# A decoder layer on one core: more of the gated layer made ahead, prompt rows weighed in pairs, sums taken from PSUM product by product

## The chip, the cores and the metric

The kernel runs on one core of a Trainium2 chip. The metric is the time on the device in microseconds. Times are given as the median of several runs, and one further execution was recorded by the profiler.

## The reference

One inference step of a decoder layer of width 2048, for one prompt of 512 new tokens and eight sample requests of 8 tokens each, 576 tokens together. The layer's input is normed by rows, `u = rms_norm(x, g_mix) @ w_in`, and `u` is shared out to three mixers: a short gated convolution (512 columns), a Mamba-2 state-space mixer (512) and sparse attention (1024). The attention has 16 query heads on 4 key heads and three branches: over compressed blocks of keys, over selected blocks and over a window of 512. A sample request has 1024 past positions in paged caches, whose raw rows are compressed by a small network. Queries and keys are normed by heads. The three outputs are normed, merged and sent through the output projection, and a gated feed-forward layer ends the step:

```
merged = concat(rms_norm(y_a), rms_norm(y_b), rms_norm(y_c))
x = x + merged @ w_out
h = rms_norm(x, g_ffn)
x = x + (silu(h @ w_gate) * (h @ w_up)) @ w_down      # d_ff = 5632
```

New cache rows, convolution tails and states are outputs as well. All data is float32.

## The kernel before

The token axis (576 columns, 288 in each half) is the free axis of nearly every matmul. A float32 product is made of three matmuls of parts: `hi` times `hi`, `hi` times `lo` and `lo` times `hi`. ScalarE makes the rounded part of a weight chunk (`whi`, `fhi`), VectorE the remainder (`wlo`, `flo`). A projection job (`run_group`, L405) makes 128 output columns from 16 row blocks: 16 x 3 x 2 = 96 matmuls of 128 x 288. There are 21 jobs for keys, values, queries and gates (`jobs1`), 12 for the state-space mixer (`jobs2`), 12 for the short convolution (`jobs3`). The two of `jobs1` that make the raw keys run while x is turned and split; `begin` also makes the row scales `rstdB` there (L334, L637), through a power on GpSimd and transposes on TensorE. The helpers record every operation under one line: L93 is ScalarE's, L96 a two-input operation, L105 one with a scalar.

Everything else of the token mixers is side work in Python generators. `Pump` (L44) holds them; each reports by `tick(ns)` a planned cost and yields. After each row block, `run_group` calls `pump.run(369.0 * halves * ratio)`, which steps generators until that much cost is used up. So ratio says how densely side work is written between projection matmuls: 0.8 for `jobs1`, 0.95 for `jobs2`, 1.1 for `jobs3` (L1653). The generator `chain` goes through the compression of the caches (`compress`, with `k_cmp_norm`, L680), sample attention, prompt attention and the merge of the attention's output (`merge_c`, L1609); `pump.drain(main)` writes what is left of it behind the last projection job. The finishing steps of projections are generators as well: `norm_T` (L467) norms a query or key by squares (ScalarE), a matmul with a block of ones, Ln and Exp on ScalarE, and one multiplication; `kv_finish` (L485) turns and stores a key or value. The framework below the kernel then places each engine's instructions in an order of its own that follows the written one loosely, and sets the semaphores.

The prompt attention (L1559) goes through four query heads `r` of a group: `turn(r)` transposes four tiles of probabilities on TensorE and copies each out of PSUM, `apply` multiplies them with values into `o`.

The gated layer (L1893) multiplies with w_gate and w_up by seven products of half-size blocks in place of eight. For each of 44 blocks `g` (gate and up by turns) and both chunks `c` of rows, matmuls (L1915) make products 1, 2, 6, 4, 3, 7, 5 into PSUM pieces P["1"] to P["7"]: 24 matmuls a product, 12 in each chunk. 1 and 2 have tiles `pt` of their own, 5 has `po`; 6 and 4 are the halves of one `pg` tile, 3 and 7 of another; only in blocks 1 to NE - 1 do 6 and 4 have `pt` tiles of their own. After the second chunk VectorE adds the pieces to `u` and `w_`, which then go through Silu, or (odd g) are multiplied on GpSimd with the Silu of the block before and stored to `g_d`. `prep(i)` splits the weights one item ahead.

For the first NE = 8 blocks products 1 and 2 are made ahead by `jobsE` (two jobs a block, 24 matmuls each) and kept in DRAM as `U_d`. Ten of these jobs (2 x NA) run while the second half of the norm is made, `norm_b` with `pair` (L1790), at ratio 0.6; the other six run inside the first item at 0.8. `pair` makes the combinations of the normed inputs that the products need, most on VectorE, three of each on GpSimd (`G`). The down projection follows; its first inputs are four stored rows, split by `g_in` into `ghl`.

The stages lie at these times of the trace (us): start to 64; projections with side work to 1142; the output projection to 1401; norm and early products to 1477; gated layer to 2401; down projection to the end.

## Time and profile before

| | us |
|---|---|
| median of 3 runs (lowest, highest) | 2980.53 (2979.23, 2984.72) |
| profiled execution | 2985.47 |
| its span | 2983.7 |
| TensorE (PE) busy | 2860.0 (96%) |
| VectorE (DVE) busy | 1942.6 (65%) |
| ScalarE (ACT) busy | 1204.7 (40%) |
| GpSimd (POOL) busy | 579.2 (19%) |

The granted clock of TensorE has a mean of 0.981. PE is the matmuls, PEld the weight loads that overlap them. The idle time of an engine that is not the bottleneck costs nothing; TensorE's idle time, wherever it lies, is time that a better order could use.

### The profile page before, as it was taken

The page shows a single profiled execution, that of the slowest core. Times are in us where ns is not written, and L with a number is a line of the kernel's source. Part 1 is how long each engine was busy: PE and PEld are TensorE (multiplying, and loading weights), DVE is VectorE, ACT ScalarE, POOL GpSimd, SP SyncE. Part 2 cuts the span into 40 slices and gives each one's busy share as a digit, 9 for nine tenths or more (in the row PEclk, how much of TensorE's full clock was granted, in tenths as well). Part 3 has the DMA queues.
Part 4 walks back from the last instruction along what each step waited for, and adds up shares of the span by engine and source line. Part 5 has one row for each costly group of instructions (what it writes and reads, how often), then busy time and mean ns, then how long its engine had stood idle before and what let it go on. Part 6 is the DMA issues. An engine that isn't in the chain of part 4 may idle for free.

```text
span 2983.7 us, 57369 instructions
## 1 busy us (share of the span) xinstructions
PE 2860.0 (96%) x22294; PEld 2756.0 (92%) x22294; DVE 1942.6 (65%) x3982; ACT 1204.7 (40%) x2287; POOL 579.2 (19%) x632
## 2 busy tenths in 40 slices
PE   7999998777999999999899999999999999999999
PEld 6989997666888899999899999999999999999999
DVE  5674774334786776668998888888888863343332
ACT  4463662222455542245544444444444431222222
POOL 3342424444343321112211110110110100000000
PEclk9999998888999999999999999999999999999999
DMA  7444434554524117366553333333333272332333
GB/s 235 121 128 126 104 81 122 151 152 153 125 54 90 49 47 196 110 199 180 158 182 124 112 108 107 109 109 108 108 108 108 83 245 86 117 114 82 96 100 94
DMA packets 476056, 364.07 MB, mean 122 GB/s; under 512 B 69738, under 2 KB 436305, under 8 KB 475785
## 3 DMA queue, kind: packets, MB, share of 16 engines
q1 hardware_dynamic: 452056, 299.99, 34.5%
q0 software_dynamic: 20944, 55.13, 6.3%
q10 hardware_dynamic: 2784, 5.29, 0.5%
q8 instruction: 176, 2.88, 0.4%
q14 instruction: 96, 0.78, 0.1%
HBM read 307.61 MB, written 50.61 MB: 120 GB/s over the span
## 4 chain that ended last, share of the span: by engine, by line
PE 55%; DVE 2%; ACT 0%; issue 0%; DMA 0%; POOL 0%; DVEq 0%; ACTq 0%; POOLq 0%; SPq 0%
PE pg L431 23%; PE pg L1915 17%; PE pt L1915 9%; PE po L1915 5%; DVE wlo L96 1%; PE pt L128 0%; DVE x L105 0%; PE pt L120 0%; DVE X L96 0%; DVE raw L96 0%; DVE x L96 0%; PE pt L431 0%; DMA raw<-in_w_gate_dram 0%; PE po L120 0%; ACT X L93 0%
## 5 line engine op out<-in xcount | busy, mean ns | idle before, releaser
L93 ACT ACTIVATE whi<-raw 128x512 fp32r<-128x512 f32 x729 | 458.1, 629 | 938.7 <-PE pg L431 575.2
L96 DVE TENSOR_TENSOR wlo<-raw,whi 128x512 fp32r<-128x512 f32 x729 | 505.5, 695 | 351.2 <-ACT whi L93 334.1
L431 PE MATMUL pg<-ghl,whi 128*128 128x288 f32 x2816 | 495.2, 296 | 2.4 <-DVE ghl L96 2.1
L431 PEld LDWEIGHTS pg<-ghl,whi 128*128 128x128 f32 x2816 | 414.9, 189 | 3.2 <-DVE ghl L96 2.8
L431 PE MATMUL pg<-hhi,whi 128*128 128x288 f32 (+1 forms) x1440 | 343.9, 320 | 9.7 <-issue 4.3
L431 PE MATMUL pg<-hlo,whi 128*128 128x288 f32 (+1 forms) x1440 | 326.2, 306 | 6.4 <-issue 4.2
L431 PE MATMUL pg<-hhi,wlo 128*128 128x288 f32 (+1 forms) x1440 | 324.1, 304 | 2.7 <-issue 2.6
L431 PE MATMUL pg<-ghl,wlo 128*128 128x288 f32 x1408 | 302.5, 296 | 0.0
L431 PEld LDWEIGHTS pg<-hhi,whi 128*128 128x128 f32 (+1 forms) x1440 | 238.0, 197 | 26.4 <-issue 20.0
L1915 PE MATMUL pt<-X,fhi 128*128 128x288 f32 x1280 | 258.5, 296 | 0.0
L431 PEld LDWEIGHTS pg<-hlo,whi 128*128 128x128 f32 (+1 forms) x1440 | 241.8, 196 | 11.8 <-issue 8.0
L1915 PE MATMUL pg<-X,fhi 128*128 128x288 f32 x1232 | 246.9, 295 | 0.8 <-ACT fhi L93 0.8
L431 PEld LDWEIGHTS pg<-hhi,wlo 128*128 128x128 f32 (+1 forms) x1440 | 241.4, 195 | 4.4 <-issue 4.0
L96 POOL TENSOR_TENSOR u<-u 128x576 f32<-128x576 f32 x44 | 69.8, 1588 | 822.8 <-DVE u L96 702.8
L431 PEld LDWEIGHTS pg<-ghl,wlo 128*128 128x128 f32 x1408 | 226.1, 189 | 0.0
L93 ACT ACTIVATE fhi<-wr 128x512 fp32r<-128x512 f32 x225 | 142.2, 632 | 189.4 <-PE pt L1915 106.4
L96 DVE TENSOR_TENSOR flo<-wr,fhi 128x512 fp32r<-128x512 f32 x225 | 197.4, 877 | 13.5 <-ACT fhi L93 11.1
L1915 PEld LDWEIGHTS pt<-X,fhi 128*128 128x128 f32 x1280 | 205.8, 188 | 0.0
L1915 PEld LDWEIGHTS pg<-X,fhi 128*128 128x128 f32 x1232 | 197.8, 188 | 1.1 <-ACT fhi L93 1.1
L431 PE MATMUL pg<-S,whi 128*128 128x288 f32 x1024 | 194.8, 298 | 0.0
L96 DVE TENSOR_TENSOR x1T<-pg,x1T 128x576 f32<-128x576 f32 x96 | 72.6, 757 | 183.0 <-PE pg L431 183.0
L1915 PE MATMUL pt<-X,flo 128*128 128x288 f32 x640 | 189.2, 296 | 0.0
(1324 smaller groups left out, 5964.3 us busy)
## 6 DMA issues: line engine op xcount, KB each, us to landing
wr<-in_w_gate_dram SPq DMA_DIRECT2D x88, 512.0 KB
wr<-in_w_up_dram SPq DMA_DIRECT2D x88, 512.0 KB
raw<-in_w_down_dram SPq DMA_DIRECT2D x176, 256.0 KB
raw<-in_w_in_dram SPq DMA_DIRECT2D x144, 256.0 KB
raw<-in_w_out_dram SPq DMA_DIRECT2D x64, 256.0 KB
g_d<-u POOLq DMA_DIRECT2D x44, 288.0 KB
u<-g_d SPq DMA_DIRECT2D x40, 288.0 KB
raw<-in_w_in_dram SPq DMA_DIRECT2D x64, 128.0 KB
```

The source lines that it names most:

```text
L93: S.activation(out, in_, func, bias=bias, scale=scale, accum_out=accum)
L96: (eng or V).tensor_tensor(out, a, b, op=op)
L431: PE.matmul(ps[:m, s, :HALF], w[:, k, :m], x[:, s * HALF:(s + 1) * HALF], start=(k0 + k == 0 and n == 0), stop=(k0 + k == n_k - 1 and n == 2))
L1915: PE.matmul(P[n], w[:, k, :], xx, start=(j == 0 and q_ == 0), stop=(j == 7 and q_ == 2))
```

## The change

It does these things:

- NE goes from 8 to 12 and NA from 5 to 8; the early jobs beside `norm_b` run at ratio 0.45 in place of 0.6, and `pair`'s three GpSimd operations go to VectorE.
- `row_scales` becomes a generator with one pause. The two raw-key jobs leave PSUM by a plain copy, and `kv_finish` multiplies by the scales when they are there.
- `norm_T` pauses twice, for 900 each, in place of once for 700.
- `k_cmp_norm` takes the power by Ln and Exp on ScalarE in place of GpSimd.
- In prompt attention, where the row has up to 256 keys, two transposed tiles share a PSUM bank and one copy, the rows are applied in pairs with two more pauses, and `o` is taken later.
- `merge_c` has all multiplications on VectorE; the ratios of `jobs2` and `jobs3` go to 0.85 and 1.05.
- In the gated layer the sums are written between the products: those of P1 and P2 after product 2, P6's after 6, P7's, P4's and P3's after 7. The last block's P5 sums, its multiplications and stores come after the first four splits of the down projection.

```diff
@@ -141,8 +141,8 @@
     SQ = 3
     PF = 3
     XSB = 2
-    NE = 8
-    NA = 5
+    NE = 12
+    NA = 8
     QLB = 1
     EVB = 5
     CRB = 5
@@ -334,7 +334,10 @@
     def row_scales():
         tt(ssq, ssq2[:, 0], ssq2[:, 1], OP.add)
         rsqrt_small(ssq, 1.0 / D)
+        tick(2500)
+        yield
         spread(rstdB, ssq)
+        ready.add("scales")
 
 
     R_GF, R_GO, R_CA, R_CB, R_BB, R_QN, R_KN, NR1 = 0, 16, 32, 44, 76, 84, 85, 88
@@ -471,8 +474,9 @@
         sq, sh, sl_ = evt(T), evt(T, F32R), evt(T, F32R)
         act(sq, u, AF.Square)
         split(sh, sl_, sq)
-        tick(700)
-        yield
+        for _ in range(2):
+            tick(900)
+            yield
         for s in range(2):
             sl = slice(s * HALF, (s + 1) * HALF)
             ps = pt()
@@ -482,7 +486,12 @@
         act(sq, sq, AF.Exp, scale=-0.5)
         stt(out, u, gain, sq, OP.mult, OP.mult)
 
-    def kv_finish(br, kv, p, u):
+    def kv_finish(br, kv, p, u, raw=False):
+        if raw:
+            while "scales" not in ready:
+                yield
+            tt(u, u, rstdB, OP.mult)
+            yield
         if kv == 0 and br > 0:
             yield from norm_T(u, cols[:, R_KN + br:R_KN + br + 1], u)
             uh, ul = evt(TP, F32R), evt(TP, F32R)
@@ -534,7 +543,12 @@
         return u
 
     def kv_job(br, kv, p):
-        return in_job(COL_KV + (br * 2 + kv) * 256 + p * 128,
+        def early(ps):
+            u = evt(T)
+            (V.tensor_copy if p else act)(v2(u), ps)
+            pump.add(kv_finish(br, kv, p, u, True))
+
+        return in_job(COL_KV + (br * 2 + kv) * 256 + p * 128, early if (br, kv) == (0, 0) else
                       lambda ps: pump.add(kv_finish(br, kv, p, evac_u(ps)), front=True))
 
     def q_finish(p, r, u):
@@ -634,7 +648,7 @@
             turn_rows()
         if ci == 3:
             squares(1)
-            row_scales()
+            pump.add(row_scales())
             for i in range(PF):
                 fetch_rows(0, i)
 
@@ -686,7 +700,8 @@
         tt(sq[:n], kc[:n], kc[:n], OP.mult)
         r4 = t1.tile([128, 4], F32, name="kcr", tag="kcr", bufs=1)
         V.reduce_sum(r4[:n], sq[:n].rearrange("p (g d) -> p g d", g=4), axis=AX)
-        rsqrt_small(r4[:n], 1.0 / 64)
+        act(r4[:n], r4[:n], AF.Ln, scale=1.0 / 64, bias=epsc[:n])
+        act(r4[:n], r4[:n], AF.Exp, scale=-0.5)
         tt(kc[:n].rearrange("p (g d) -> p g d", g=4), kc[:n].rearrange("p (g d) -> p g d", g=4),
            r4[:n, :, None].to_broadcast([n, 4, 64]), OP.mult)
         return kc
@@ -1532,6 +1547,18 @@
 
                 def turn(r):
                     out = []
+                    if W <= 256:
+                        ss_ = st.pop(r)
+                        for k0 in (0, 2):
+                            ps = pt()
+                            for k in (k0, k0 + 1):
+                                for t_ in range(nk):
+                                    c = (k - k0) * W + t_ * 128
+                                    tp(ps[:, c:c + 128], ss_[k][:, t_ * 128:(t_ + 1) * 128], ident)
+                            pT = pp.tile([128, 512], F32, name="pT", tag="pT", bufs=5)
+                            (act if k0 else V.tensor_copy)(pT[:, :2 * W], ps[:, :2 * W])
+                            out += [pT[:, :W], pT[:, W:2 * W]]
+                        return out
                     for k, s_ in enumerate(st.pop(r)):
                         ps = pt()
                         for t_ in range(nk):
@@ -1558,14 +1585,11 @@
                     tp(ps[:, h * 128:(h + 1) * 128], pc[:, h].rearrange("q r n -> q (r n)"), ident)
                 pcT = pp.tile([128, 256], F32, name="pcT", tag="pcT", bufs=1)
                 act(pcT, ps[:, :256])
-                for _ in range(2):
+                for _ in range(4 if W <= 256 else 2):
                     tick(700)
                     yield
-                o = po()
-                for r in range(4):
-                    for h in range(2):
-                        mm(o[h * 64:(h + 1) * 64, r * 128:(r + 1) * 128], VCb[:, 2 * p + h, r, :], pcT[:, h * 128:(h + 1) * 128],
-                           start=(r == 0), stop=False)
+                o = None
+                held = []
                 for r in range(4):
                     pTs = turn(r)
                     yield
@@ -1577,7 +1601,17 @@
                     else:
                         tick(700)
                         yield
-                    apply(o, r, pTs)
+                    held.append((r, pTs))
+                    if W <= 256 and r % 2 == 0:
+                        continue
+                    if o is None:
+                        o = po()
+                        for r_ in range(4):
+                            for h in range(2):
+                                mm(o[h * 64:(h + 1) * 64, r_ * 128:(r_ + 1) * 128], VCb[:, 2 * p + h, r_, :],
+                                   pcT[:, h * 128:(h + 1) * 128], start=(r_ == 0), stop=False)
+                    while held:
+                        apply(o, *held.pop(0))
                     yield
                 act(qT[:, p * 4:(p + 1) * 4, qs], o.rearrange("d (r q) -> d r q", r=4))
 
@@ -1613,7 +1647,7 @@
         yield from rms_bcast(sq_c, 1024)
         for k in range(8):
             tick(1500)
-            merge(qT[:, k, :], sq_c, cols[:, R_GO + 8 + k:R_GO + 9 + k], S4[:, k], S4[:, 8 + k], G if k in (3, 5, 7) else V)
+            merge(qT[:, k, :], sq_c, cols[:, R_GO + 8 + k:R_GO + 9 + k], S4[:, k], S4[:, 8 + k], V)
             yield
 
     def merge_a():
@@ -1651,8 +1685,8 @@
     add_jobs(jobs2 + jobs3)
     main = pump.add(chain())
     run_jobs(jobs1[2:], 0.8)
-    run_jobs(jobs2, 0.95)
-    run_jobs(jobs3, 1.1)
+    run_jobs(jobs2, 0.85)
+    run_jobs(jobs3, 1.05)
     pump.drain(main)
     close_pool(kpg)
     close_pool(hig)
@@ -1795,18 +1829,18 @@
         tick(800)
         yield
         norm_half(1, i)
-        tt(xh_(0, j), xh_(1, i), xh_(1, j), OP.subtract, G)
+        tt(xh_(0, j), xh_(1, i), xh_(1, j), OP.subtract)
         tt(t2_, xh_(1, i), t1_, OP.subtract)
         put(6, j, t2_)
         tick(1170)
         yield
         tt(xh_(0, i), t2_, xh_(0, i), OP.subtract)
         put(4, j, xh_(0, i))
-        put(3, j, xh_(1, i), G)
+        put(3, j, xh_(1, i))
         tick(740)
         yield
         X[7].append(slot(1, j, F32R))
-        put(7, j, xh_(0, j), G)
+        put(7, j, xh_(0, j))
         X[5].append(slot(0, j, F32R))
         put(5, j, t1_)
         tick(370)
@@ -1884,7 +1918,7 @@
     flags = set()
     X[5], X[7] = [], []
     pump.add(norm_b())
-    run_jobs(jobsE[:2 * NA], 0.6)
+    run_jobs(jobsE[:2 * NA], 0.45)
     while 0 not in flags:
         pump.step()
     load(2)
@@ -1913,25 +1947,27 @@
                 j = c * KC + k
                 for q_, (w, xx) in enumerate(((hi, x[j][:, 0]), (hi, x[j][:, 1]), (lo, x[j][:, 0]))):
                     PE.matmul(P[n], w[:, k, :], xx, start=(j == 0 and q_ == 0), stop=(j == 7 and q_ == 2))
+            if c and n == "2":
+                U[g] = evt(T)
+                act(U[g][:, HALF:], P["1"])
+                tt(U[g][:, :HALF], P["2"], U[g][:, HALF:], OP.add)
+            elif c and n == "6":
+                u, w_ = U.pop(g), evt(T)
+                tt(u[:, HALF:], P["6"], u[:, HALF:], OP.add)
+            elif c and n == "7":
+                tt(w_[:, HALF:], P["7"], u[:, HALF:], OP.add)
+                tt(w_[:, :HALF], w_[:, HALF:], P["4"], OP.subtract)
+                tt(u[:, HALF:], P["3"], u[:, HALF:], OP.add)
         if i == 0:
             run_jobs(jobsE[2 * NA:], 0.8)
             pump.drain()
             for _ in prep(1):
                 pass
             load(3)
-        if c == 0:
+        if c == 0 or i == len(items) - 1:
             continue
-        if g >= NE:
-            U[g] = evt(T)
-            act(U[g][:, HALF:], P["1"])
-            tt(U[g][:, :HALF], P["2"], U[g][:, HALF:], OP.add)
-        u, w_ = U.pop(g), evt(T)
-        tt(u[:, HALF:], P["6"], u[:, HALF:], OP.add)
-        tt(w_[:, HALF:], P["7"], u[:, HALF:], OP.add)
-        tt(w_[:, :HALF], w_[:, HALF:], P["4"], OP.subtract)
         tt(w_[:, HALF:], P["5"], w_[:, HALF:], OP.add)
         tt(u[:, HALF:], P["5"], u[:, HALF:], OP.add)
-        tt(u[:, HALF:], P["3"], u[:, HALF:], OP.add)
         if g % 2 == 0:
             act(u, u, AF.Silu)
             act(w_, w_, AF.Silu)
@@ -1992,6 +2028,11 @@
         nc.sync.dma_start(g0[:, f_], g_d[f_])
     for f_ in range(4):
         g_in(f_, g0[:, f_])
+
+    for q_, (a, b) in enumerate(zip((u, w_), sil)):
+        tt(a[:, HALF:], P["5"], a[:, HALF:], OP.add)
+        tt(a, a, b, OP.mult, G)
+        nc.gpsimd.dma_start(g_d[nf - 2 + q_], a)
     for m in range(4):
         nc.sync.dma_start(x1T[:, m], x1_d[m])
     for n, j in enumerate(jobs6):
```

## Rows read from the trace of the kernel before

**Rows 1.** The page: span, TensorE's busy time (share of the span, instructions), and by line the chain that ended last.

```profile
span 2983.7 us, 57369 instructions
...
PE 2860.0 (96%) x22294; PEld 2756.0 (92%) x22294; DVE 1942.6 (65%) x3982; ACT 1204.7 (40%) x2287; POOL 579.2 (19%) x632
...
PE pg L431 23%; PE pg L1915 17%; PE pt L1915 9%; PE po L1915 5%; DVE wlo L96 1%; PE pt L128 0%; DVE x L105 0%; PE pt L120 0%; DVE X L96 0%; DVE raw L96 0%; DVE x L96 0%; PE pt L431 0%; DMA raw<-in_w_gate_dram 0%; PE po L120 0%; ACT X L93 0%
```

**Rows 2.** The windows, two of 100 us. Columns: window, its length; busy us (and instructions) of PE, PEld, DVE, ACT, POOL; granted clock of PE, DMA share, GB/s.

```profile
500.00:600.00 100.00, 80.09 (x773) 64.54 (x771) 42.16 (x119) 23.39 (x43) 46.09 (x46) 0.88 0.50 152
...
1400.00:1500.00 100.00, 88.67 (x623) 83.03 (x622) 89.61 (x158) 52.74 (x108) 25.67 (x25) 1.00 0.50 153
```

**Rows 3.** The windows, columns as in rows 2: the key norm's place, sample attention, prompt attention, and the gated layer behind its start.

```profile
280.00:290.00 10.00, 6.53 (x27) 5.38 (x27) 2.46 (x4) 1.77 (x4) 5.12 (x6) 0.62 0.36 96
540.00:770.00 230.00, 188.83 (x1889) 158.04 (x1890) 97.66 (x283) 57.53 (x109) 98.08 (x103) 0.89 0.50 151
785.00:1085.00 300.00, 294.36 (x2415) 260.85 (x2416) 224.87 (x787) 157.71 (x441) 103.60 (x109) 1.00 0.28 66
1500.00:2394.00 894.00, 894.00 (x6730) 894.00 (x6729) 746.44 (x1181) 387.78 (x638) 91.17 (x84) 1.00 0.36 113
```

**Rows 4.** The waits, 0 to 480 us, TensorE alone: engine, output and line that waited, what ended the wait; us in total, times, longest.

```profile
PE pg L431 <- DVE u L96: 2.3, 1, 2.3
...
PE pt L128 <- POOL ssq L96: 0.5, 1, 0.5
```

**Rows 5.** The timeline of GpSimd's queue, a gather of the start: start, length, engine, line, operation [idle before it].

```profile
67.83 0.97 POOL L271 DMA_INDIRECT cr<-in_cache_k_dram,idxC  x1 [0.30 <-issue]
```

**Rows 6.** The waits of rows 4's view, other rows of it.

```profile
PE pt L120 <- ACT u L93: 5.2, 4, 1.4
...
PE pt L120 <- DVE xl L96: 0.7, 1, 0.7
```

**Rows 7.** The timeline from 272 us, all engines, at the norm of the last 32 compressed keys; columns as in rows 5.

```profile
283.86 1.05 POOL L96 TENSOR_TENSOR kcr<-kcr,mhalf 32x4 f32<-32x4 f32 x1
...
284.94 0.41 DVE L96 TENSOR_TENSOR kcn<-kcn,kcr 32x256 f32<-32x256 f32 x1 [8.75 <-issue]
```

**Rows 8.** The timeline of ScalarE at the first norm of a key: the two table loads, ahead of the Ln at 127.94 and of the Exp at 131.04.

```profile
126.65 1.28 ACT L93 ACT_TABLE_LOAD   x1
...
129.74 1.28 ACT L93 ACT_TABLE_LOAD   x1
```

**Rows 9.** The waits of all engines, 520 to 770 us.

```profile
POOL vp L271 <- PE po L120: 72.3, 8, 11.9
```

**Rows 10.** The timeline at the end of the token part: GpSimd's and VectorE's work of `merge_c`, and the last projection matmuls on TensorE.

```profile
1098.80 4.96 POOL L96 TENSOR_TENSOR qT<-qT,sq_c 128x576 f32<-128x576 f32 x3 [1.50 <-ACT sq_c L93]
...
1116.94 0.81 DVE L105 SCALAR_TENSOR_TENSOR S<-qT,cols,S 128x576 fp32r<-128x576 f32 x1
...
1142.42 0.70 PE L431 MATMUL pg<-S,whi 128*128 128x288 f32 x4
```

**Rows 11.** The windows at the start of the gated layer, columns as in rows 2: its whole start, one of its 10 us, and blocks 1 to 7.

```profile
1401.50:1481.50 80.00, 68.67 (x472) 63.03 (x471) 71.46 (x126) 41.21 (x88) 25.67 (x25) 1.00 0.48 147
1411.50:1421.50 10.00, 7.27 (x47) 6.21 (x47) 10.00 (x18) 5.18 (x12) 4.00 (x5) 1.00 0.43 128
1481.50:1604.00 122.50, 122.50 (x927) 122.50 (x927) 116.64 (x191) 54.59 (x90) 17.06 (x16) 1.00 0.54 168
```

**Rows 12.** The groups of instructions of 1401 to 1480 us, one of GpSimd's three, then VectorE's of the same shape (first and last of the five slower ones, and the fast one): line, engine, operation, out<-in, shape, count; busy us, mean ns; idle before.

```profile
L96 POOL TENSOR_TENSOR x<-x 128x288 f32<-128x288 f32 x8 | 8.6, 1081 | 18.2 <-DVE raw L96 18.2
...
L96 DVE TENSOR_TENSOR X<-raw,X 128x288 fp32r<-128x288 f32 x8 | 6.7, 832 | 0.0
...
L96 DVE TENSOR_TENSOR X<-x,X 128x288 fp32r<-128x288 f32 x8 | 4.2, 524 | 0.2 <-ACT X L93 0.2
L96 DVE TENSOR_TENSOR raw<-x,x 128x288 f32<-128x288 f32 x8 | 3.6, 451 | 0.1
```

**Rows 13.** The timeline of the gated layer's last block, TensorE and VectorE: the last matmul of product 2 and the read of P2, the last of product 6, the last of product 4, and the read of P6.

```profile
2393.07 0.29 PE L1915 MATMUL pt<-X,flo 128*128 128x288 f32 x1
...
2393.47 0.46 DVE L96 TENSOR_TENSOR u<-pt,u 128x288 f32<-128x288 f32 x1 [1.99 <-PE pt L1915]
...
2394.66 0.30 PE L1915 MATMUL pg<-X,flo 128*128 128x288 f32 x1
...
2396.24 0.29 PE L1915 MATMUL pg<-X,flo 128*128 128x288 f32 x1
...
2396.58 0.46 DVE L96 TENSOR_TENSOR u<-pg,u 128x288 f32<-128x288 f32 x1 [2.64 <-PE pg L1915]
```

**Rows 14.** The timeline of TensorE in the gated layer's first item.

```profile
1442.35 0.40 PE L1915 MATMUL po<-x,flo 128*128 128x288 f32 x1 [0.20 <-DVE flo L96]
...
1444.22 0.53 PE L1915 MATMUL pg<-X,whi 128*128 128x288 f32 x2 [0.28 <-ACT whi L93]
...
1445.44 0.43 PE L431 MATMUL pt<-X,whi 128*128 128x288 f32 x2
1445.71 0.30 PE L1915 MATMUL pg<-X,wlo 128*128 128x288 f32 x1
```

**Rows 15.** The timeline at the border to the down projection, VectorE and TensorE.

```profile
2401.47 0.82 DVE L96 TENSOR_TENSOR u<-po,u 128x288 f32<-128x288 f32 x2
...
2404.15 0.53 PE L431 MATMUL pg<-ghl,whi 128*128 128x288 f32 x2 [2.13 <-DVE ghl L96]
```

## Prediction

> **What bounds the kernel now.** I read the busy table and the chain that ended last first. TensorE is busy 2860.0 of 2983.7 us, and most of the chain that ended last is its matmuls, so about 124 us of idle TensorE (2983.7 - 2860.0) are nearly all that a better order can win [rows 1]. The windows say where they lie: 1500 to 2394 has none, 500 to 600 has 20 us, 1400 to 1500 11 us [rows 2, 3]. Where TensorE idles the granted clock is lower too (0.88 in 500 to 600, 0.62 in 280 to 290) [rows 2, 3]: an idle microsecond there can cost more than itself. Then I took each place that the diff touches and asked in the waits and the timeline what ends last there.
>
> **The change part by part.** A minus is a gain.
>
> *Row scales put off, first kv jobs leave PSUM raw.* Now the jobs behind the start wait for the scales: a matmul 2.3 us for VectorE's `u`, a transpose 0.5 us for GpSimd's `ssq` [rows 4]. Both go: -2.8. The power on GpSimd will stand behind the six gathers that `begin` issues after it, each 0.97 + 0.30 us [rows 5], so the scales come about 6 x 1.27 + 2.5 (the tick) = 10 us later. The next job that needs them lasts 96 x 0.133 = 12.8 us (894.00 us for 6730 matmuls is 0.133 each [rows 3]) and covers that narrowly. I take -3; bounds -5 (a lower clock right after the wait goes too) and 0 (the next evacuation waits instead).
>
> *Norm of q and k with two ticks.* Four times TensorE waited at the norm's matmul for the squares on ScalarE, 5.2 us in all, and 0.7 us for a split [rows 6]. One more yield puts a further stretch of projection matmuls ahead of it. -5; bounds -7 (with gaps laid to issue beside it) and +1 (the norm ends later and holds its buffers longer).
>
> *Key norm by logarithm.* The 32-row norm waited 8.75 us on VectorE because its power, 1.05 us of work, stood on GpSimd behind gathers until 283.86 [rows 7]. TensorE lost 3.47 us in 280 to 290, at clock 0.62 [rows 3], but a weight split on ScalarE came late there as well, so I count -2. Against it: there are five such norms, and a Ln with its Exp brings two table loads of 1.28 us [rows 8]: 5 x 2.56 = 12.8 us of ScalarE. Bounds: -9 (the whole wait) and +6 (half of the 12.8 delays `whi` and through it TensorE).
> The Trainium skill's "ScalarE: Activation LUTs", section "Table sets: the hidden batching unit", counts ln and then exp as one table load, since one set holds both. The trace disagrees: a load stands at 126.65 ahead of the norm's Ln and another at 129.74 ahead of its Exp [rows 8]. By the page the loads would be 6.4 us and the upper bound +3.
>
> *Ratios 0.95 to 0.85 and 1.1 to 1.05.* In sample attention TensorE is busy 188.83 of 230 us at clock 0.89 [rows 3]; what ends last is a chain of small steps (GpSimd's `vp` gathers wait 72.3 us for TensorE's `po`) [rows 9]. A lower ratio puts more projection between the steps. The planner takes 32 x 369 ns = 11.8 us for a job, so 12 x 0.1 x 11.8 = 14.2 us and 12 x 0.05 x 11.8 = 7.1 us of side work move later. If all of the 14.2 us filled idle time it would be -12; if the steps only stretch, 0. I take the middle, -6.
>
> *End of the token part.* This eats slack: `merge_c` ended on VectorE at 1116.94 + 0.81 = 1117.75, and projections run to 1142.4, 25 us later [rows 10]. Out of it go 14.2 + 7.1, two more ticks of 700 ns for each of four turns of the prompt (5.6) and some 2 us of the norms' ticks: 29. So `drain` may find a few us of side work with nothing beside it. POOL's three multiplications of `merge_c`, 4.96 us [rows 10], go to VectorE, which does the like in 0.8 us. I take 0; bounds -4 (POOL's late tail goes) and +8 (29 - 25, twice, for the wait on `S` behind it).
>
> *Prompt rows in pairs.* Half the copies out of PSUM, and one more turn of scores ahead. TensorE loses 5.64 us in 785 to 1085 [rows 3]; -2, bounds -6 (all) and +1.
>
> *Start of the gated layer.* From 1401.5 to 1481.5 TensorE is busy 68.67 us and 472 matmuls are shown, 62.8 us at 0.133; VectorE is busy 71.46, in one window 10.00 of 10 [rows 11]. So 11.3 to 17.2 us are lost. Four more blocks made ahead bring 8 jobs of 24 matmuls, 25.5 us, which blocks 8 to 11 no longer have. The 24 POOL operations of about 1.0 us become VectorE's at 0.45: +10.8. But five groups of eight operations on VectorE take 0.83 down to 0.52 us beside POOL where one takes 0.45; their 8.0 us of excess should go back [rows 12]. Eight jobs add 8 x 2 x 0.69 for splits and 4 x 0.45 for sums, 12.8. VectorE: 71.5 + 10.8 - 8.0 + 12.8 = 87.1; TensorE: 88 to 94. Both fit in 95, against 80 + 25.5 = 105.5 now: -10; bounds -16 and 0. Blocks 8 to 11 then run as blocks 1 to 7 do: VectorE 116.64 of 122.5 us, TensorE full [rows 11]. Four more loads and stores of `U` on SP's queue lie among its weights.
>
> *Sums that leave PSUM product by product.* The adds are the same; where they stand among the matmuls changes. P6 and P4 are the two halves of one `pg` tile. In the last block the matmuls of product 6 ended at 2394.96, yet VectorE, idle for 2.64 us, read P6 at 2396.58, as product 4 ended at 2396.53; P2, alone in its tile, was read as its own matmuls ended [rows 13]. So a read is ordered against the whole tile. Now P6's read is written before the second half of product 4, which writes that tile: product 4 may not begin before it. This holds in blocks 12 to 43 and in block 0, 33 times (in 1 to 11 the two have tiles of their own). The whole price is the read 0.46, a split of 0.69 ahead of it on a VectorE busy 83% (746.44 of 894 [rows 3]), and a restart of about 0.22 (0.20 and 0.28 where TensorE waited on an operand [rows 14]): 1.37 x 33 = 45. Behind the wait stands the rest of the block on TensorE's queue; only the written order can put something between. It does elsewhere: matmuls of L431 are laid between those of L1915 at 1445.44 [rows 14]. If product 3 takes that place, the restart is left: 0.22 x 33 = 7. I take +7; bounds 0 and +45.
>
> *Last block's P5 sums after four splits.* At 2404.15 TensorE had waited 2.13 us for the first `ghl`, which stood behind two P5 adds of 0.82 us together [rows 15] and the reads of P7 and P4 before them. P7 and P4 leave earlier now, the P5 adds later. The two stores put off carry the rows that the down projection reads last. -3; bounds -4 and 0.
>
> Sum: -3 -5 -2 -6 +0 -2 -10 +7 -3 = -24. The profiled execution took 2985.5 us, the median of the runs is 2980.5, 5 less; from the median 2980.5 - 24 = 2957.
>
> **The rivals.**
> 1. *No wait at P6 at all.* The written order may hide it all, or only the tile's half count. -24 - 7 = -31: 2950. Against it: the late read at 2396.58 [rows 13]. 0.20. The Trainium skill's "PSUM — Partial Sum Buffer", section "🎯 Summary: rules for kernel authors", says that a read beside a running matmul wants a different bank and is guarded by bank; by that the halves would not order each other. The trace's read of P6, held for product 4, speaks against it here.
> 2. *TensorE waits at every P6 read* (the slower side). -31 + 45 = +14: 2994. For it: reads are ordered by the tile; against it: matmuls of other products are laid between elsewhere. The sign turns at 31 / 33 = 0.94 us a block. 0.13.
> 3. *The gated layer's start stays bound by VectorE.* It is at 10.00 of 10 in a window and gets more; if the 8.0 us do not come back, nothing is won there: -24 + 10 = -14: 2966. 0.12.
> 4. *Side work runs past the projections.* Sample attention gives 0 in place of -6 and the end costs 8: -24 + 6 + 8 = -10: 2970. For it: 29 us out of a slack of 25. 0.10.
>
> **How the numbers follow.** The forecast, 2957, has 0.45; its own range, from the terms' distances to their nearer bounds added as squares (2, 2, 7, 6, 4, 3, 6, 7, 1 give 14), is 2943 to 2971. The whole range goes from rival 1 less 14 to rival 4 plus 14, 2936 to 2984, rounded to 2985; it leaves out most of rival 2. 0.2%, 6 us, is about what measurements of this kernel can tell. Faster: 0.44 of the forecast, 0.20, 0.09 of rival 3, 0.05 of rival 4: 0.78. Same: 0.01, 0.03 and 0.04 of these and 0.01 of rival 2: 0.09. Slower: 0.12 of rival 2 and 0.01 of rival 4: 0.13.
>
> **What would show it.** Right: no wait of TensorE on `u` near 62; the waits on the squares gone; TensorE above 84% in sample attention; in the first 90 us of the gated layer VectorE near full and TensorE above 90%; P6 read as product 6 ends, with gaps on TensorE beside it below 0.3 us. Wrong: some 1.4 us of idle TensorE in every block after the twelfth, so 94% in windows after 1750 (rival 2); TensorE idle between the last projection and `w_out` (rival 4).

## Result and the profile after

The changed kernel takes 3005.82 us (median of 4 runs, 3000.35 to 3005.98); the kernel before took 2981.46 in the same session. The ratio is 1.0072, interval 1.0057 to 1.0087: slower by 0.7%, where 0.8% faster was forecast. It lies outside the range, on the side of rivals 2 and 4, and past the prices of both (2994 and 2970). The profiled execution has a span of 3004.1 us.

The experiments ran on several chips of two kinds. On the first kind, which is that of the result, the kernel before takes 2970 to 2981 us; on the second kind it takes some 2883. So every ratio is against runs on its own chip.

The page of the changed kernel answers to [rows 1]: TensorE's busy time is the same within 1 us, so over the whole kernel nearly all of the 20.4 us of span are idle time of TensorE.

```profile
span 3004.1 us, 57413 instructions
...
PE 2861.0 (95%) x22294; PEld 2756.2 (92%) x22294; DVE 1944.5 (65%) x4005; ACT 1216.3 (40%) x2276; POOL 540.9 (18%) x600
...
PE pg L434 23%; PE pg L1949 16%; PE pt L1949 9%; PE po L1949 5%; PE pt L434 1%; PE pt L128 0%; DVE wlo L96 0%; PE pt L120 0%; DMA raw<-in_w_gate_dram 0%; DVE x L105 0%; DMA raw<-in_w_up_dram 0%; DVE X L96 0%; DMA h<-in_state_ssm_dram 0%; DVE raw L96 0%; PE po L120 0%
```

Where they lie is read from the first and last matmul of each stage in the two traces (L431 is now L434, L1915 is L1949):

| us | before | changed | |
|---|---|---|---|
| first job of jobs2 | 485.9 | 476.2 | -9.7 |
| first gather of sample attention | 465.7 | 493.7 | +28.0 |
| last VectorE operation of `merge_c` ends | 1117.75 | 1158.55 | +40.8 |
| first w_out matmul | 1142.4 | 1147.8 | +5.4 |
| output projection (from its first w_out matmul) lasts | 257.7 | 278.1 | +20.4 |
| norm, early products and gated layer last | 1001.4 | 997.0 | -4.4 |
| down projection lasts | 577.2 | 576.1 | -1.1 |

The last four lines are stages, and they add up: 5.4 + 20.4 - 4.4 - 1.1 = 20.3. The projections of `jobs2` begin sooner, the side chain (`chain`: compression, sample and prompt attention, `merge_c`) ends 41 us later, and where the two meet, in the output projection, the time is lost: TensorE is idle there for 16.7 us where it was idle for 3.9, and the other 7.6 us are more busy time, at the lower clock shown below. The windows (columns as in rows 2) of the changed kernel, first 500 to 600, which answers to [rows 2], then around the first w_out matmul, and last the early products, which answer to [rows 11]:

```profile
500.00:600.00 100.00, 73.60 (x610) 58.01 (x609) 38.65 (x98) 19.13 (x35) 44.90 (x46) 0.80 0.51 157
...
1100.00:1200.00 100.00, 86.49 (x655) 81.23 (x654) 62.46 (x155) 38.34 (x74) 6.56 (x9) 0.91 0.45 126
1150.00:1160.00 10.00, 5.10 (x29) 4.87 (x28) 9.67 (x19) 3.53 (x6) 3.01 (x4) 0.83 0.94 273
1170.00:1180.00 10.00, 4.70 (x23) 4.22 (x24) 5.56 (x29) 0.23 (x2) 0.00 (x0) 0.60 0.78 201
1180.00:1190.00 10.00, 8.81 (x49) 8.06 (x48) 5.00 (x17) 3.64 (x9) 2.22 (x2) 0.72 0.58 161
1426.00:1520.00 94.00, 90.11 (x645) 86.12 (x644) 80.20 (x167) 53.25 (x109) 1.18 (x1) 1.00 0.59 180
```

The kernel before, same view, same stretches of its trace (its w_out begins 5.4 us sooner):

```profile
1100.00:1200.00 100.00, 96.32 (x741) 94.02 (x740) 73.69 (x171) 34.27 (x58) 17.29 (x17) 0.98 0.60 167
1150.00:1160.00 10.00, 10.00 (x80) 9.73 (x79) 5.49 (x18) 2.83 (x5) 2.42 (x3) 1.00 1.07 341
```

Before, TensorE was full in 1150 to 1160; `merge_c` had ended 24.7 us ahead of the first w_out matmul. Now TensorE has 5.10 and 4.70 of 10 in two windows, and the clock is 0.60 and 0.72 in and after the second. What it waits for there, in the waits of TensorE and in the timeline of VectorE and TensorE:

```profile
PE pt L120 <- DVE sd L105: 6.6, 1, 6.6
PE pg L434 <- DVE wlo L96: 4.9, 1, 4.9
```

```profile
1155.84 2.71 DVE L105 SCALAR_TENSOR_TENSOR S<-qT,cols,S 128x576 fp32r<-128x576 f32 x2
...
1168.71 0.46 DVE L96 TENSOR_TENSOR x<-pg,x 128x288 f32<-128x288 f32 x1 [5.04 <-PE pg L434]
1169.09 0.19 DVE L96 TENSOR_TENSOR sd<-dtg,dtb 128x40 f32<-128x40 f32 x1
...
1155.38 0.85 PE L434 MATMUL pg<-S,wlo 128*128 128x288 f32 x2 [4.90 <-DVE wlo L96]
...
1175.30 0.64 PE L120 MATMUL pt<-sd,triU 128*128 128x32 f32 x2 [6.62 <-DVE sd L105]
```

One job's weights (`wlo`) stand on VectorE among the last multiplications of `merge_c`, which is still at work at 1155.84. Then come the first steps of the state-space scan, 25 small operations on `sd` of some 0.2 us one after another, from 1169.09 to 1175.24, and a matmul waits 6.62 us for them. VectorE is not too busy for them: they stand behind an operation that empties a w_out job's PSUM (`x<-pg,x`), for which VectorE itself was idle for 5.04 us. Before, `merge_c` and these steps were over by 1127.5, under the projections; the timeline of the kernel before has the last of them at

```profile
1127.26 0.20 DVE L105 SCALAR_TENSOR_TENSOR sd<-sd,ea 128x40 f32<-128x40 f32 x1
```

### The profile page after: what moved, and what is told of

The parts are those of the page before. It is cut to its first block, busy times and chain, and to the rows that moved or that the text cites. A ratio compares the mean times of both kernels' runs of the same rounds, so it can differ in the third digit from the quotient of the medians.

```text
span 3004.1 us, 57413 instructions
## 1 busy us (share of the span) xinstructions
PE 2861.0 (95%) x22294; PEld 2756.2 (92%) x22294; DVE 1944.5 (65%) x4005; ACT 1216.3 (40%) x2276; POOL 540.9 (18%) x600
## 4 chain that ended last, share of the span: by engine, by line
PE 55%; DVE 1%; DMA 1%; ACT 0%; issue 0%; POOL 0%; SPq 0%; DVEq 0%; ACTq 0%
PE pg L434 23%; PE pg L1949 16%; PE pt L1949 9%; PE po L1949 5%; PE pt L434 1%; PE pt L128 0%; DVE wlo L96 0%; PE pt L120 0%; DMA raw<-in_w_gate_dram 0%; DVE x L105 0%; DMA raw<-in_w_up_dram 0%; DVE X L96 0%; DMA h<-in_state_ssm_dram 0%; DVE raw L96 0%; PE po L120 0%
## 5 line engine op out<-in xcount | busy, mean ns | idle before, releaser
L93 ACT ACTIVATE whi<-raw 128x512 fp32r<-128x512 f32 (+1 forms) x606 | 380.5, 629 | 824.4 <-PE pg L434 555.8
L96 DVE TENSOR_TENSOR wlo<-raw,whi 128x512 fp32r<-128x512 f32 (+1 forms) x606 | 418.7, 692 | 330.4 <-ACT whi L93 296.8
L434 PE MATMUL pg<-ghl,whi 128*128 128x288 f32 x2816 | 494.2, 296 | 2.4 <-DVE ghl L96 2.4
L434 PEld LDWEIGHTS pg<-ghl,whi 128*128 128x128 f32 x2816 | 413.9, 188 | 3.1 <-DVE ghl L96 3.1
L434 PE MATMUL pg<-hhi,whi 128*128 128x288 f32 (+1 forms) x1440 | 344.2, 318 | 7.2 <-issue 6.7
L1949 PE MATMUL pg<-X,fhi 128*128 128x288 f32 x1656 | 333.5, 297 | 0.4 <-DVE u L96 0.4
L434 PE MATMUL pg<-hlo,whi 128*128 128x288 f32 (+1 forms) x1440 | 325.4, 306 | 7.4 <-issue 4.9
L434 PE MATMUL pg<-hhi,wlo 128*128 128x288 f32 (+1 forms) x1440 | 324.0, 306 | 6.7 <-issue 3.6
L434 PE MATMUL pg<-ghl,wlo 128*128 128x288 f32 x1408 | 302.1, 295 | 0.0
L1949 PEld LDWEIGHTS pg<-X,fhi 128*128 128x128 f32 x1656 | 264.8, 188 | 4.4 <-DVE u L96 0.6
L434 PEld LDWEIGHTS pg<-hhi,whi 128*128 128x128 f32 (+1 forms) x1440 | 237.1, 196 | 22.1 <-issue 18.8
L434 PEld LDWEIGHTS pg<-hhi,wlo 128*128 128x128 f32 (+1 forms) x1440 | 241.6, 196 | 12.4 <-issue 8.9
L434 PEld LDWEIGHTS pg<-hlo,whi 128*128 128x128 f32 (+1 forms) x1440 | 241.4, 195 | 11.7 <-issue 7.7
L93 ACT ACTIVATE fhi<-raw 128x512 fp32r<-128x512 f32 x246 | 155.3, 632 | 212.4 <-PE pg L1949 180.9
L1949 PE MATMUL pg<-X,flo 128*128 128x288 f32 x828 | 239.3, 295 | 0.0
L1949 PE MATMUL pt<-X,whi 128*128 128x288 f32 x1168 | 235.8, 295 | 0.0
L434 PEld LDWEIGHTS pg<-ghl,wlo 128*128 128x128 f32 x1408 | 225.6, 188 | 0.0
L96 DVE TENSOR_TENSOR flo<-raw,fhi 128x512 fp32r<-128x512 f32 x246 | 170.2, 693 | 46.2 <-ACT fhi L93 41.9
L434 PE MATMUL pg<-S,whi 128*128 128x288 f32 x1024 | 196.2, 300 | 0.4 <-DVE u L96 0.4
L1949 PEld LDWEIGHTS pt<-X,whi 128*128 128x128 f32 x1168 | 188.2, 188 | 0.0
```

The costliest lines, as they stand in the source:

```text
L93: S.activation(out, in_, func, bias=bias, scale=scale, accum_out=accum)
L96: (eng or V).tensor_tensor(out, a, b, op=op)
L434: PE.matmul(ps[:m, s, :HALF], w[:, k, :m], x[:, s * HALF:(s + 1) * HALF], start=(k0 + k == 0 and n == 0), stop=(k0 + k == n_k - 1 and n == 2))
L1949: PE.matmul(P[n], w[:, k, :], xx, start=(j == 0 and q_ == 0), stop=(j == 7 and q_ == 2))
```

## Experiments

The theory on record ahead of the first runs, called late chain in the expectations: the side chain is late. What was put off in the first 480 us, and the lower ratios, move the token side work behind the projections. Rivals: sample attention itself lost by the changed token parts, and TensorE's wait at P6.

**The ratios back.**

```diff
-    run_jobs(jobs2, 0.85)
-    run_jobs(jobs3, 1.05)
+    run_jobs(jobs2, 0.95)
+    run_jobs(jobs3, 1.1)
```

> The changed kernel with the ratios of jobs2 and jobs3 back at 0.95 and 1.1. Late-chain theory (the token side work ends after the projections, so that the output projection's first 60 us run with nothing beside the small steps; 20.4 us of the loss lie there): the last merge_c operation comes before the first w_out matmul again by 5 to 15 us, the output projection takes about 260 us in place of 278, and the time is 2985 (2978 to 2992). Rival (the loss is in sample attention itself, through the put-off scales, the norms' ticks or the log norm): above 2997.

Measured 0.9987 (0.9978 to 0.9997) of the kernel before; `merge_c` ends 13 us ahead of w_out, the output projection takes 262.5 us. The absolute time does not apply, as this chip is of the second kind; both signs of the theory are there.

**One tick in norm_T.**

```diff
-        for _ in range(2):
-            tick(900)
-            yield
+        tick(700)
+        yield
```

> The changed kernel with norm_T back at one tick of 700. Late-chain theory: the compression is finished with the projections of jobs1 again, sample attention starts some 20 us earlier than in the changed kernel (493.7 there), the chain ends before the last projection by about 5 us; 2990 (2982 to 2997), the first 480 us slower by up to 5. Rival (ratios alone did it): 3004 or more.

0.9989 (0.9979 to 0.9998). The first gather is at 464.2, 14 us sooner than in the changed kernel on that chip, but `merge_c` ends 0.8 us behind the first w_out matmul, not ahead, and the output projection takes 277.4. The gain came in the projections' end (1023.8 for 1030.4). So only part of the expectation held.

**The ratios alone**, the reverse of the first diff on the kernel before, run twice.

> The kernel before with only the ratios at 0.85 and 1.05. Late-chain theory: merge_c ends just before the last projection, so nothing is gained and up to 12 us lost: 2987 (2979 to 2993). Forecast's own step (sample attention gains 6, the slack of 25 us holds): 2975.

> The kernel before with only the ratios at 0.85 and 1.05, once more: 9 us slower where the kernel before takes 2883 us. Late-chain theory: again 8 to 14 us slower, of them 10 to 14 in the output projection and some back before it. If TensorE idles in sample attention on this chip (kernel before near 2975), the forecast's step of 6 us gained should show in the projections' end at least.

1.0033 (1.0019 to 1.0048) and 1.0044 (1.0030 to 1.0058). The output projection takes 271.4 and 271.3 us for 257.8 to 258.3; the waits of TensorE there, in the second run, begin with the same row:

```profile
PE pt L120 <- DVE sd L105: 3.5, 1, 3.5
PE pg L431 <- ACT whi L93: 2.3, 1, 2.3
```

Both chips were of the second kind, so what the ratios win where TensorE idles in sample attention was not seen alone.

**The changed kernel and the kernel before, on chips of the second kind.**

> The changed kernel itself, to stand beside the variants on their chip, where the kernel before takes 2883 us. Late-chain theory: slower than the variants with the ratios or the tick back (0.9987, 0.9989) by 0.4 to 0.8%, so 1.003 to 1.007 of the kernel before. Rival (the variants gain by the chip alone): 0.999.

> The kernel before, for its trace on this chip: sample attention without the stalls of the first chip (TensorE near 99% in 500 to 660 us), merge_c 20 to 25 us ahead of the last projection, the output projection in 258 us. If the first chip's stalls came from the kernel and not the chip, they are here again.

> The kernel before, for its trace on this chip: sample attention's first gather 8 to 20 us ahead of the first job of jobs2, merge_c's end 24 us ahead of the first w_out matmul, 258 us for the output projection.

The changed kernel takes 1.0025 (1.0013 to 1.0037). Its windows (columns as in rows 2) at its first w_out matmul, 1030.4:

```profile
1030.00:1040.00 10.00, 4.73 (x29) 4.21 (x28) 10.00 (x20) 4.25 (x8) 2.84 (x3) 0.86 0.79 236
...
1050.00:1060.00 10.00, 3.39 (x24) 3.16 (x23) 6.01 (x28) 0.44 (x2) 0.00 (x0) 0.88 0.65 172
1060.00:1070.00 10.00, 9.27 (x45) 8.13 (x45) 3.21 (x15) 1.82 (x6) 2.22 (x2) 0.50 0.44 116
```

The kernel before has TensorE at 10.00, 10.00 and 9.04 of 10 in these windows. The output projection takes 280.4 for 257.8, so the loss there is 22.6 us (20.4 on the first chip), but the projections end 6.0 us sooner (1030.4 for 1036.4). The kinds of chip differ in sample attention: on this kind TensorE is nearly full there (500 to 600, kernel before, which on the first chip had 80.09 and clock 0.88 [rows 2]):

```profile
500.00:600.00 100.00, 99.58 (x1262) 86.61 (x1261) 58.28 (x161) 35.62 (x68) 71.96 (x71) 1.00 0.76 233
```

Put in order by the end of `merge_c` against the first w_out matmul (minus is ahead; how far ahead is called the lead), the output projection lasts:

| kernel | `merge_c` ends, us | output projection, us |
|---|---|---|
| before (first chip; second kind) | -24.7; -24.5 | 257.7; 257.8 |
| the two ticks alone, twice | -23.6; -23.7 | 259.1; 259.1 |
| prompt rows in pairs alone | -19.3 | 257.8 |
| ratios and tick back | -18.6 | 258.0 |
| ratios back | -12.8 | 262.5 |
| ratios alone | -4.4; -4.5 | 271.4; 271.3 |
| one tick | +0.8 | 277.4 |
| changed (first chip; second kind) | +10.8; +10.8 | 278.1; 280.4 |

A lead of 18.6 us costs next to nothing yet; at 12.8 us 4.7 are lost, and from there each microsecond of lead that goes costs about one, until some 20 are lost. So of the lead of 24.7 us only some 7 are free to spend (an estimate: by the slope between these rows the loss begins at some 17). The rest covers what VectorE has to do behind `merge_c`: the scan's first steps end 15.0 us ahead of w_out in the kernel before, 6.6 ahead with ratios and tick back, 2.6 ahead with the ratios back, and 27.5 behind it in the changed kernel. The rows are of several kernels and of both kinds of chip.

**Ratios and tick back together**, both diffs.

> The changed kernel with both the ratios and the norm's single tick back. Late-chain theory: merge_c ends some 20 us ahead of the last projection, the output projection takes 258 to 260 us, and the gated layer keeps its 6 us: 2874 (2869 to 2879), ratio 0.997. Rival (the other token parts cost 4 us by themselves, as the sums up to the end of the output projection in the two runs with one of them back hint: 1302 and 1301 against 1294 to 1299): 2880, ratio 0.999.

1.0010 (1.0000 to 1.0019), the rival's side: the output projection is whole again (258.0), and still nothing is won. The trace of the kernel with the gate and border parts alone (below, same chip) tells where: against it this one is 13.7 us longer, 6.1 of them before w_out (1133.2 for 1127.1), 5.9 in the gated layer, where the sums between the products stand, and 1.5 in the down projection. Its first gather is at 476.5 for 463.3, though the tick is back. Which part puts that off is not shown. With the row scales alone, on a chip of the second kind, the first gather is at 470.1, for 458.4 and 464.9 in two kernels with the code of before up to there; the scales were not tried alone on the first kind, so they stay a suspect.

**The two ticks alone** on the kernel before, twice, on chips where it takes 2970.

> The kernel before with only norm_T's two ticks of 900. Forecast's step: 5 us faster. Late-chain theory: the projections of jobs1 end some 10 us earlier, sample attention starts some 15 us later, nothing is won: merge_c 10 us ahead of the last projection, output projection 260 to 264 us, time 2883 (2879 to 2887).

> The kernel before with only norm_T's two ticks, once more. If the loss is the later start of sample attention on a chip where TensorE idles there: 12 us slower again near 2971, but only 0 to 4 us where the kernel before takes 2883. If the ticks cost by themselves: 10 to 14 on either.

1.0044 (1.0028 to 1.0060) and 1.0069 (1.0046 to 1.0091). The output projection lasts 259.1 us both times, so here nearly all of the loss is ahead of it. In the first run the first job of jobs2 starts at 467.5, the first gather at 477.5; in the kernel with the gate and border parts alone (same chip, same token part as before) they are at 476.4 and 463.3, and w_out begins there at 1127.1, here at 1141.0. The first gathers, of the ticks alone and then of the gate and border parts, in the timeline of GpSimd:

```profile
477.52 0.97 POOL L271 DMA_INDIRECT kp<-in_cache_k_dram,idxS  x1 [0.15 <-issue]
```

```profile
463.31 0.97 POOL L271 DMA_INDIRECT kp<-in_cache_k_dram,idxS  x1 [0.15 <-issue]
```

From the first gather to the end of `merge_c` both take the same: 1117.3 - 477.5 = 639.8 and 1102.4 - 463.3 = 639.1. So in this pair the chain sets the time where sample attention stalls, and its start 14 us later is paid at the end. The second run does not bear out that the length is fixed: from 476.69 to 1125.84 its chain takes 649.2 us, where the kernel with gate, border and logarithm on that chip takes 639.4; 11 us of it are sample attention (282.7 us from first gather to last for 271.7). Why is not shown. On the second kind of chip the ticks alone were not tried.

**Prompt rows in pairs alone; row scales alone; key norm by logarithm alone**, each on the kernel before. Their diffs are those parts of the change, nothing else.

> The kernel before with only the prompt rows in pairs (shared banks, two more ticks). Forecast's step: 2 us faster. Late-chain theory: 5.6 us of ticks move the chain some 6 us later out of 24, which costs 0 to 3 us in the output projection: 2883 (2880 to 2886).

> The kernel before with only the row scales as a generator and the two raw-key jobs taken out of PSUM raw. Forecast's step: 3 us faster. Theory now (whatever is put off in the first 480 us starts sample attention's gathers later, and their ramp of 16 gathers is then no longer under the last projections of jobs1): the first w_out matmul 0 to 6 us later, 1.000 to 1.002.

> The kernel before with only the key norm's power by Ln and Exp. Forecast's step: 2 us faster, 0.9993. If ten table loads of 1.28 us stand in the way of weight splits: 2 to 6 us slower. The first gather of sample attention tells the two apart: earlier, or 3 to 10 us later.

1.0003 (0.9993 to 1.0014), 1.0006 (0.9996 to 1.0015), 0.9987 (0.9978 to 0.9997). In profiles taken on the second kind of chip the positions of the token part differ by some 5 us between kernels whose token part is the same (w_out at 1036.4 and 1041.7), and the first gather by 6.5, so smaller shifts are not read from them. The 6.0 and 6.6 us read above from the end of the projections are hardly above this.

**The gated layer's start alone.**

```diff
-    NE = 8
-    NA = 5
+    NE = 12
+    NA = 8
...
-    run_jobs(jobsE[:2 * NA], 0.6)
+    run_jobs(jobsE[:2 * NA], 0.45)
```

and `pair`'s three operations on VectorE.

> The kernel before with only the early part of the gated layer changed (12 blocks, 8 pairs of jobs first, ratio 0.45, VectorE for the three GpSimd operations). Forecast's step: 10 us faster (6 to 16), ratio 0.9965. Rival 3 of the forecast (VectorE-bound, nothing won): 1.000.

0.9958 (0.9943 to 0.9974); the stage takes 989.9 us for 1001.2. Its window:

```profile
1299.00:1393.00 94.00, 90.77 (x649) 86.65 (x649) 80.45 (x168) 53.00 (x109) 1.18 (x1) 1.00 0.59 180
```

**The sums between the products alone**, and the changed kernel without them.

> The kernel before with only the gated sums written between the products (P5's last sums left in place). Small waits theory: 2 to 5 us slower, ratio 1.0007 to 1.0017. Rival (TensorE waits at each P6 read, here in 37 blocks): over 1.010. Nothing at all: 1.000.

> The changed kernel with the gated sums back behind all products and the last block's sums back ahead of the first splits. If the waits for P6 cost little, as the windows after 1600 us suggest (749 matmuls in 100 us for 754, about 0.13 us a block): 3004 (3000 to 3008), 4 us gained in the blocks and 2 lost at the border. If TensorE waits at every P6 read (my rival): 2965.

1.0017 (1.0007 to 1.0027) alone; the gated stage takes 1005.3 us for 1001.2. Without them the changed kernel comes to 1.0005 (0.9995 to 1.0015), against 1.0025 with them. The windows of the blocks, the sums alone and then the kernel before, both on chips of the second kind:

```profile
1500.00:2290.00 790.00, 790.00 (x5914) 785.54 (x5914) 654.37 (x1020) 342.65 (x564) 74.39 (x70) 1.00 0.33 106
```

```profile
1500.00:2290.00 790.00, 790.00 (x5945) 790.00 (x5944) 644.50 (x1018) 342.67 (x564) 73.75 (x68) 1.00 0.33 106
```

31 matmuls fewer in 790 us, 31 x 0.133 = 4.1 us, for about 35 blocks: 0.12 us each.

**The best of it: the gated layer's start and the last block's P5 sums put off**, and then with the logarithm too.

> The kernel before with the early part of the gated layer (gate_alone) and the last block's P5 sums behind the first four splits, and nothing else: gate_alone's 12 us and up to 3 at the border: 2869 (2866 to 2872), ratio 0.995. If the border gives nothing: 2871.

> The kernel before with the early part of the gated layer, the last block's P5 sums put off and the key norm by logarithm: the gains add if they are independent, 0.9957 times 0.9987 = 0.9944 (0.993 to 0.996). If the log norm gave its 2 us by chance: 0.9957.

0.9957 (0.9944 to 0.9970): 2957.73 us where the kernel before takes 2971.35, faster than both kernels. The gate alone gave 0.9958, so what the border adds can't be told; in this kernel P3's sum also goes ahead of P5's in every block. With the logarithm 0.9978 (0.9966 to 0.9991), above the expected sum of the gains. That was another chip, where the gate and border were not run without it, so the log norm's own 0.13% stays unsettled.

## Why the prediction was wrong, point by point

- **End of the token part: 0, bounds -4 and +8.** This is the step that failed, in size. The direction was there (rival 4: 29 us out of a slack of 25), but its price in the output projection was 20.4 us, not 8. I took the whole slack as free and priced only what runs past it (29 - 25, twice); the runs show that only some 7 of the 25 us were free, since the weight splits and the first steps of the scan that stand on VectorE behind `merge_c` lost their cover as well. With 7 free, 29 us would have come to some 22 (an estimate). The 29 was short too: the lead fell by 35.4 us, from 24.7 ahead to 10.8 behind. The ratios took 20.1 of it alone, where I had 21.3, and the pairs 5.4, where I had 5.6, but the norms' ticks took from 1.0 (alone) to 10.0 (one tick against the changed kernel), where I had 2. And the idle time lies inside the output projection, not ahead of w_out, where my sign for rival 4 looked for it.
- **Ratios, -6.** No gain. Alone they cost 9 to 13 us on the chips tried, all in the output projection (+13.6). Between sample attention's first gather and its last the first chip took 284.7 us before and 283.3 after, with 787 projection matmuls in it before and 748 after: the gaps took up no more of the projections. TensorE is busy there for 77% of the time, where my sign was above 84%. The ticks changed with it; the ratios alone were not tried on a chip of this kind.
- **Norm of q and k, -5.** The waits did change, but their sum did not fall; in the changed kernel's waits (0 to 480 us, TensorE, against the 5.2 us and 0.7 us of [rows 6]) the one on the squares is smaller, and another has come:

```profile
PE pt L128 <- DVE xl L96: 4.6, 4, 2.6
PE pt L120 <- ACT u L93: 3.5, 3, 1.4
```

  But the norm's time was not the point: the ticks push the compression behind the last projection of `jobs1`. Before, sample attention's first gathers, 16 in a row at some 1.27 us as in [rows 5], began 20 us ahead of jobs2's first job and ran under the last of `jobs1`; now they begin 18 us behind it. The timeline of GpSimd, before and then changed, has the first of them at

```profile
465.69 0.97 POOL L271 DMA_INDIRECT kp<-in_cache_k_dram,idxS  x1 [0.15 <-issue]
```

```profile
493.73 0.97 POOL L271 DMA_INDIRECT kp<-in_cache_k_dram,idxS  x1 [0.15 <-issue]
```

  Alone the ticks cost 0.44% and 0.69% on the first kind of chip.
- **Row scales, -3; prompt pairs, -2; key norm, -2.** Scales and pairs: no change that can be told. Key norm: 0.13% faster alone, not kept beside the gate. Its ten table loads came as counted, two for each of five norms (26 in the kernel before):

```profile
L93 ACT ACT_TABLE_LOAD x36 | 46.2, 1283 | 6.1 <-DMA xt<-in_x_prompt_dram 5.5
```

- **Start of the gated layer, -10.** Right: 11.3 us in the stage, ratio 0.9958. TensorE has 90.8 of 94 us. VectorE's operations came back to 0.45 us with GpSimd's gone, against 0.83 and 0.52 [rows 12]; the groups of instructions of the changed kernel, 1426 to 1520:

```profile
L96 DVE TENSOR_TENSOR X<-x,X 128x288 fp32r<-128x288 f32 x16 | 7.0, 450 | 0.0
...
L96 DVE TENSOR_TENSOR X<-raw,X 128x288 fp32r<-128x288 f32 x8 | 3.6, 452 | 0.0
L96 DVE TENSOR_TENSOR raw<-x,x 128x288 f32<-128x288 f32 x8 | 3.6, 452 | 0.1
```

  Rival 3 falls by this.
- **Sums by product, +7, bounds 0 and +45.** Right in kind, 4 us: 0.12 a block, where I had 0.22. The wait on the tile is real and mostly filled, as the timeline of the changed kernel (TensorE, VectorE, a block's P6; against [rows 13]) shows:

```profile
2393.92 0.43 PE L1949 MATMUL pg<-X,fhi 128*128 128x288 f32 x2
...
2394.12 0.46 DVE L96 TENSOR_TENSOR u<-pg,u 128x288 f32<-128x288 f32 x1 [0.36 <-PE pg L1949]
2394.19 0.30 PE L1949 MATMUL pg<-X,flo 128*128 128x288 f32 x1
...
2394.33 0.84 PE L1949 MATMUL pg<-X,fhi 128*128 128x288 f32 x4
...
2394.87 0.19 PEld L1949 LDWEIGHTS pg<-X,flo 128*128 128x128 f32 x1
```

  P6 is read at 2394.12, right behind product 6's last matmul, and until 2394.58. A product goes `fhi`, `fhi`, `flo`, so in the group of four `fhi` at 2394.33 one product leaves off and the next begins: the first two, of another product, run during the read, and by the group's length (0.84, where four take 0.70 [rows 10]) the other two start after it. So a little over 0.1 us is left a block, against the 1.37 of rival 2. Rivals 1 and 2 both fall; the Trainium skill's rule of a different bank ("PSUM — Partial Sum Buffer", "🎯 Summary: rules for kernel authors") does not describe this kernel's order, which goes by the tile (P6 read only at 2396.58 in the kernel before [rows 13]).
- **Border, -3.** The one wait of 2.13 us [rows 15] became three of 2.40 together:

```profile
2424.32 0.53 PE L434 MATMUL pg<-ghl,whi 128*128 128x288 f32 x2 [0.69 <-DVE ghl L96]
...
2426.22 0.54 PE L434 MATMUL pg<-ghl,whi 128*128 128x288 f32 x2 [0.44 <-DVE ghl L96]
...
2428.55 0.54 PE L434 MATMUL pg<-ghl,whi 128*128 128x288 f32 x2 [1.27 <-DVE ghl L96]
```

  `ghl`'s splits still come one by one from VectorE beside GpSimd's multiplications, as before: the first takes 0.75 us where it took 1.88, but the other three take 4.62 together where they took 3.30. The stage is 1.1 us shorter all the same; in the windows, before and then changed, the clock behind the waits is 1.00 where it was 0.83, which goes the same way, but its share was not worked out:

```profile
2405.00:2415.00 10.00, 9.89 (x64) 9.55 (x63) 6.67 (x9) 2.64 (x4) 1.99 (x2) 0.83 0.99 351
```

```profile
2425.00:2435.00 10.00, 8.29 (x60) 7.82 (x60) 8.15 (x9) 2.20 (x4) 3.14 (x4) 1.00 1.01 347
```

- **The sum.** My terms of the token part gave -18; the runs gave +26 on the first chip and +16.6 on the second kind. The gated terms gave -6, the runs -5.5 and -7.4.

## What to carry to other kernels

Where side work is written between matmuls by a planner's costs, look at which of the two streams sets the end, and at the lead that one has over the other at the place where they meet: putting work off is free only for the part of that lead that covers nothing else (here some 7 of 25 us), and it must be counted for every edit that spends it, together. A wait that goes on the main engine is no gain if the work put off with it starts a longer chain later. Try the parts of a large change one by one: here one of them, the gated layer's start, carried nearly all of the gain that the runs can tell.

## What was not expected of the hardware

The same kernel takes 2883 us on two chips, 2970 and 2971 on two others and 2981 in the session of the result, and nearly all of the difference is sample attention: first gather to last, 191.7 us (458.5 to 650.2) against 284.7 (465.7 to 750.4), with the same number of instructions. Where it is long, TensorE, ScalarE and VectorE stand idle there in many pieces with no releaser that the profile shows ("issue", or "remote" where the profile has no instruction for it). Three rows of the waits of the kernel before on the first chip, 540 to 720 us:

```profile
PE po L120 <- issue: 14.1, 15, 3.1
...
ACT pT L93 <- remote: 21.2, 5, 7.0
...
DVE ss L96 <- remote: 7.0, 1, 7.0
```

TensorE's granted clock is lower there as well, 0.88 against 1.00 in 500 to 600; which of the two follows from the other is not shown. What causes it was not found. It changes what an edit is worth: the changed kernel is at 1.0072 on the one kind of chip and at 1.0025 on the other.
